# FFN up projection by one level of Strassen's algorithm, down projection accumulated over all of k in PSUM

## The chip, the cores and the metric

The kernel runs on one core of one Trainium2 chip. Its time is device microseconds of one execution. Three runs of the kernel before gave a median of 1679.16 us.

## The reference, cut to what matters

One decoder layer on 1024 tokens with a model width of 1024. A first part (modulated LayerNorm, gated linear attention and sliding-window attention side by side, output projection, LayerNorm) makes `x`. The change concerns what follows:

```python
h2 = layer_norm(x) * (1.0 + scale2) + shift2
u = h2 @ w_up[l]                                  # (1024, 1024) @ (1024, 5632)
up = jnp.pad(u, ((0, 0), (CONV_W - 1, 0), (0, 0)))
u = conv_b[l] + sum(conv_w[l, t] * up[:, t:t + S] for t in range(CONV_W))
u_gate, u_val = jnp.split(u, 2, axis=-1)          # 2816 each
f = jax.nn.gelu(u_gate, approximate=False) * u_val
x = layer_norm_affine(ALPHA * x + gate2 * (f @ w_down[l]), ln2_g[l], ln2_b[l])
```

## The kernel before, in words

**Precision.** Every large product is made of three matmuls: each operand is split into a high part `hi` (rounded to fp32r by a copy) and a low part `lo` (the difference), and hi·hi, hi·lo and lo·hi are accumulated. For weights, `Stream.emit_to` (L236) loads a 128x512 piece into `wst` (4 buffers), ScalarE writes `whi` (L250), VectorE writes `wlo` (L251); of each of these there are 8 buffers. For activations `to_half` does the same after a transpose (L392 to L401): ScalarE applies the modulation, VectorE copies hi, POOL subtracts lo.

**Order of TensorE.** It is written out by hand: `unit` (L329) issues the matmuls of one product, eight k tiles with three matmuls each, and after each k tile `run_due` issues what `at` has deferred until a running estimate of TensorE's time has passed. Within the other engines a scheduler orders instructions when the kernel is built, by their place in the program and by when their inputs should be ready.

**Before the FFN.** The last output projection (`o_unit` with 512 columns, 8 token tiles) is followed per token tile by `ln_a` (the first LayerNorm, into `x1[t]`) and `ln_b` (the normed copy `xn2[t]`). `h2_part` then makes `h2`, the transposed and split input, in two halves of 512 tokens. `ada_part(3, kt)` accumulates gate2 on VectorE (L603, L605: 16 pieces of 128x512), 2.5 us apart on the estimate.

**FFN.** The 2816 hidden units are 22 tiles of 128. `up_part(i, hf)` makes the gate and value products of tile i for one half of the tokens: two times 24 matmuls of 128x512, with the result in PSUM. `conv` reads PSUM: ScalarE takes the last tap and the bias (L1091), VectorE the other two (L1093, L1096); then Gelu (L1115), the product (L1118) and the split of f into `fh` (ScalarE, L1119) and `fl` (POOL, L1120). `down_piece` (L1130) multiplies f of one tile by its down weights for one token tile and one half of the columns: three matmuls into a PSUM bank, which VectorE adds to `x1` (L1145). The 16 pieces of tile v-2 are laid between the matmuls of `up_part(v)`. The down weights are multiplied by gate2 on POOL (L248) before they are split. The last three tiles (`N_LAST`) share one accumulation per piece and run at the end, each token tile followed by `finish` (L1147): the second LayerNorm on VectorE, its rstd on POOL (L369, L370), one scaling on ScalarE (L1158), one addition on POOL (L1159) and the store. SBUF keeps `x1` throughout, in the 8 buffers `y`.

```python
        for j in range(2):
            if tags is not None:
                us[i, j, hf] = ps1(tags)
            elif hf == 0:
                w2 = ps2()
                us[i, j, 0], us[i, j, 1] = w2[:, 0:512], w2[:, 512:1024]
            ch_unit(h2, hf, up_id[i], slice(128 * j, 128 * j + 128), us[i, j, hf], lambda: evac(j))
```

PSUM has 8 banks: two `pj`, two `m`, and two `w2` of two banks each.

Of the kernel before, what the change touches and what calls it, by code (L numbers as in the profile page):

```python
# [9 lines left out]
F32 = mybir.dt.float32  # L10
# [8 lines left out]
P = 128  # L19
S = 1024  # L20
# [12 lines left out]
N_LAST = 3  # L33
MOD_PE = 1
ADA3_D = 10.0
# [6 lines left out]
# ------------------------------------------------------------------ host layout  # L42
# [19 lines left out]
def _layout(a):  # L62
# [44 lines left out]
    return dict(x=a["x"][0], pos=pos, wlra=wlra, wbig=wbig, wdn=wdn, ada1=ada1, ada2=ada2, cst=cst, pv=pv, sm=sm,  # L107
# [3 lines left out]
_NAMES = ["x", "pos", "wlra", "wbig", "wdn", "ada1", "ada2", "cst", "pv", "sm", "lr", "rows"]  # L111


# ------------------------------------------------------------------ device program
@with_exitstack
def hybrid_layer_kernel(ctx: ExitStack, tc: tile.TileContext, x, pos, wlra, wbig, wdn, ada1, ada2, cst, pv, sm, lr,
# [9 lines left out]
    sq = ctx.enter_context(tc.tile_pool(name="sq", bufs=3))  # L126
    ps = ctx.enter_context(tc.tile_pool(name="ps", bufs=2, space=PSUM))
# [10 lines left out]
    sm_sb = cp.tile([P, 16 + 8 + 256], F32, name="sm_sb")  # L138
    pos_sb = cp.tile([P, NT], I32, name="pos_sb")
# [4 lines left out]
    ccum = cp.tile([P, 256], F32R, name="ccum")  # L144
# [12 lines left out]
    ring = cp.tile([P, P], F32, name="ring")  # L157
# [3 lines left out]
    diag = cp.tile([P, P], F32, name="diag")  # L161
# [14 lines left out]
    # ---------------- silu(c)  # L176
# [47 lines left out]
    # ---------------- weight stream  # L224
    class Stream:
# [988 lines left out]
```

## Time and profile before

| | us |
|---|---|
| three runs | 1677.97, 1679.16, 1681.36 |
| span of the profiled execution | 1677.0 |
| first matmul of the FFN | 916.7 |
| start of the last matmul | 1662.7 |

The profiled execution's own time is shown as its span, from its first to its last instruction; the median of the runs is 2.2 us above it. On the timelines a row gives start, duration, engine, line, operation, output and inputs, shape and count, and in brackets the idle time before it and what ended that. Neighbouring instructions of one engine overlap a little in these records, so the pitch from start to start is shorter than the duration.

### The profile page before, as it was taken

What the parts mean: (1) busy time and instruction counts of PE and PEld (TensorE: products, weight loads), DVE (VectorE), ACT (ScalarE), POOL (GpSimd) and SP (SyncE); (2) the same over time, 40 slices, a digit from 0 to 9 for tenths busy, and PEclk for the clock granted to TensorE, in tenths of its full rate; (3) what the DMA queues carried; (4) which work ended last, traced back from release to release, by engine and by line L of the source; (5) the groups of instructions that cost most, each with busy time, mean ns of one, the idle gap of its engine ahead of it and who ended that gap; (6) DMA issues with size and microseconds to landing.
All of it is one profiled execution on the core that took longest, in us unless ns stands there. A gap on an engine that the chain in (4) does not pass through costs nothing.

```text
span 1677.0 us, 28106 instructions
## 1 busy us (share of the span) xinstructions
PE 1619.8 (97%) x10777; PEld 1433.1 (85%) x10778; DVE 1079.8 (64%) x2278; ACT 658.6 (39%) x1590; POOL 504.0 (30%) x702
## 2 busy tenths in 40 slices
PE   5899999999999999999998899999999999999996
PEld 4899999998999989989996688888888888888885
DVE  7766666675645545536658876666666666666658
ACT  5565555554535544445313433222322222232222
POOL 5523222232623614415216521111111111111217
PEclk9999999999999999999999999999999999999998
DMA  7501000114123032111141422111211121112112
GB/s 245 163 24 36 27 27 27 33 46 121 57 61 116 27 101 89 52 51 33 51 131 39 139 68 65 44 39 46 62 44 38 51 63 39 38 50 64 38 38 101
DMA packets 58761, 108.28 MB, mean 65 GB/s; under 512 B 6641, under 2 KB 9201, under 8 KB 58626
## 3 DMA queue, kind: packets, MB, share of 16 engines
q1 hardware_dynamic: 58626, 106.49, 21.0%
q8 instruction: 84, 1.38, 0.3%
q14 instruction: 51, 0.42, 0.1%
HBM read 102.27 MB, written 4.19 MB: 63 GB/s over the span
## 4 chain that ended last, share of the span: by engine, by line
PE 86%; DVE 6%; POOL 4%; ACT 1%; issue 1%; DMA 1%; SPq 0%; DVEq 0%; POOLq 0%; ACTq 0%
PE pj L346 10%; PE pj L348 10%; PE pj L347 10%; PE w L361 9%; PE w L363 9%; PE w L362 9%; PE m L1139 6%; PE pj L1139 6%; DVE acc L530 2%; PE m L719 2%; PE pj L361 2%; PE pj L362 2%; PE pj L363 2%; PE m L758 2%; POOL y L1159 1%
## 5 line engine op out<-in xcount | busy, mean ns | idle before, releaser
L346 PE MATMUL pj<-whi,hh 128*128 128x256 f32 (+1 forms) x1296 | 373.2, 288 | 0.0
L348 PE MATMUL pj<-whi,hl 128*128 128x256 f32 (+1 forms) x1296 | 366.9, 283 | 0.0
L347 PE MATMUL pj<-wlo,hh 128*128 128x256 f32 (+1 forms) x1296 | 366.7, 283 | 0.0
L361 PE MATMUL w<-h2h,whi 128*128 128x512 f32 x672 | 266.7, 397 | 0.0
L362 PE MATMUL w<-h2l,whi 128*128 128x512 f32 x672 | 263.9, 393 | 1.0 <-POOL h2l L401 1.0
L363 PE MATMUL w<-h2h,wlo 128*128 128x512 f32 x672 | 264.4, 393 | 0.0
L346 PEld LDWEIGHTS pj<-whi,hh 128*128 128x128 f32 x1296 | 248.3, 192 | 0.6 <-issue 0.2
L347 PEld LDWEIGHTS pj<-wlo,hh 128*128 128x128 f32 x1296 | 246.5, 190 | 0.6 <-issue 0.2
L348 PEld LDWEIGHTS pj<-whi,hl 128*128 128x128 f32 x1296 | 246.1, 190 | 0.0
L251 DVE TENSOR_TENSOR wlo<-wst,whi 128x512 fp32r<-128x512 f32 (+1 forms) x200 | 145.2, 737 | 96.4 <-ACT whi L250 95.3
L1120 POOL TENSOR_TENSOR fl<-cv,fh 128x512 fp32r<-128x512 f32 x44 | 57.3, 1302 | 488.1 <-ACT fh L1119 473.3
L250 ACT CAST whi<-wst 128x512 fp32r<-128x512 f32 (+1 forms) x208 | 127.2, 620 | 152.9 <-DMA wst<-in_wbig 106.3
L362 PEld LDWEIGHTS w<-h2l,whi 128*128 128x128 f32 x672 | 126.7, 189 | 31.7 <-POOL h2l L401 1.8
L363 PEld LDWEIGHTS w<-h2h,wlo 128*128 128x128 f32 x672 | 126.4, 188 | 30.6
L361 PEld LDWEIGHTS w<-h2h,whi 128*128 128x128 f32 x672 | 126.4, 188 | 29.7 <-issue 0.2
L1145 DVE TENSOR_TENSOR y<-y,m 128x512 f32<-128x512 f32 x152 | 104.0, 684 | 71.7 <-PE m L1139 69.8
L1091 ACT ACTIVATE cv<-w,pv_sb 128x512 f32<-128x512 f32 x84 | 65.3, 777 | 214.6 <-PE w L363 214.2
L1093 DVE SCALAR_TENSOR_TENSOR cv<-w,pv_sb,cv 128x511 f32<-128x511 f32 (+1 forms) x168 | 125.2, 745 | 33.6 <-ACT cv L1091 32.3
L1145 DVE TENSOR_TENSOR y<-y,pj 128x512 f32<-128x512 f32 x152 | 104.2, 685 | 65.5 <-PE pj L1139 65.4
L248 POOL TENSOR_TENSOR wst<-wst,gate 128x512 f32<-128x512 f32 x44 | 58.7, 1338 | 79.6 <-DMA wst<-in_wdn 56.3
L698 POOL TENSOR_SCALAR_AFFINE_SELECT pch<-ph 128x512 f16<-128x512 f16 x32 | 20.5, 640 | 195.0 <-ACT ph L693 195.0
L675 ACT ACTIVATE ss<-ss,nm 128x128 f32<-128x128 f32 x128 | 49.9, 391 | 39.7 <-DVE nm L672 39.7
(402 smaller groups left out, 3526.2 us busy)
## 6 DMA issues: line engine op xcount, KB each, us to landing
wst<-in_wbig SPq DMA_DIRECT2D x200, 256.0 KB, 2.8
aw<-in_ada SPq DMA_DIRECT2D x96, 256.0 KB, 3.3
wst<-in_wdn SPq DMA_DIRECT2D x44, 256.0 KB, 2.6
y<-in_x SPq DMA_DIRECT2D x8, 512.0 KB, 9.0
out<-y SPq DMA_DIRECT2D x16, 256.0 KB, 2.0
xt<-in_x SPq DMA_DIRECT2D x8, 256.0 KB, 2.6
th<-in_x SPq DMA_DIRECT2D x13, 128.0 KB, 2.1
wst<-in_wlra SPq DMA_DIRECT2D x4, 272.0 KB, 2.7
```

Source lines behind the costliest of these rows:

```text
L250: act.copy(out=hi, in_=st)
L251: lo_eng.tensor_tensor(out=lo, in0=st, in1=hi.bitcast(F32), op=ALU.subtract)
L346: pe.matmul(acc, lhsT=lh, rhs=wh, start=kt == 0 if start is None else start, stop=False)
L347: pe.matmul(acc, lhsT=lh, rhs=wl, start=False, stop=False)
L348: pe.matmul(acc, lhsT=ll, rhs=wh, start=False, stop=kt == NK - 1 if stop is None else stop)
L361: pe.matmul(acc, lhsT=wh, rhs=ah[:, :, kt, :], start=(kt == 0), stop=False)
L362: pe.matmul(acc, lhsT=wh, rhs=al[:, :, kt, :], start=False, stop=False)
L363: pe.matmul(acc, lhsT=wl, rhs=ah[:, :, kt, :], start=False, stop=(kt == NK - 1))
L1091: act.activation(out=c_, in_=u, func=AF.Identity, scale=wv[:, 2:3], bias=bv)
L1093: dve.scalar_tensor_tensor(out=c_[:, lag:512], in0=u[:, 0:512 - lag], scalar=wv[:, 2 - lag:3 - lag], in1=c_[:, lag:512], op0=ALU.mult, op1 ...
L1139: pe.matmul(acc, lhsT=l_[:, ts_], rhs=r_[:, 0, :], start=(n == 0), stop=(n == 3 * len(blk) - 1))
L1145: dve.tensor_tensor(out=xs, in0=xs, in1=acc, op=ALU.add)
```

## The change

Twenty of the 22 gate/value tile pairs (all but the first two, `N_CLASSIC`) take Strassen's algorithm on 2x2 blocks: gate and value channels are the two column blocks, k tiles 0-3 and 4-7 the blocks of k, the two token halves the blocks of tokens. There are seven products (`product`, four k tiles with three matmuls each) per tile in place of eight such blocks. `combine` makes the sums of activation blocks (`tt_[2..4]`; a fourth is written over `h2`, `t1f`) once; `up_step` makes the sums of weight blocks per tile on POOL and splits seven weight operands; `tile_of` adds the products up, into `ug` and `uv` in SBUF. The convolution now works on 1024 tokens at a time and reads SBUF. f is written to HBM (`fd`), x1 too (`x1d`). A second stage then reads f and the down weights for each half `s` of the tokens and accumulates all 22 tiles in 8 PSUM banks, four token tiles by two column halves; `finish` multiplies by gate2. The modulation pieces `ada_part(3, kt)` start at 60 and come 6 us apart. Some constants get a pool of their own that is closed before the FFN; nothing else changes ahead of it.

```diff
-N_LAST = 3
+N_CLASSIC = 2
+B_FIRST = 3
-ADA3_D = 10.0
+ADA3_D = 60.0
+ADA3_P = 6.0
 ADA_D = 5.0
 LN_D = 5.0
 H2_D, H2_P = 12.0, 1.5
...
     wdn = a["w_down"][0].reshape(NFF, P, 2, 512).transpose(0, 2, 1, 3)
...
+    fd = tc.dram_tile([NFF, P, S], F32, name="fd")
     ps = ctx.enter_context(tc.tile_pool(name="ps", bufs=2, space=PSUM))
...
         for w_ in ids:
...
+        sp.dma_start(x1d[t], z)
...
+        keep = None
+        if hf == 1:
+            if kt % 2 == 0:
+                b1f.append(yp.tile([P, D], F32, name="b1f", tag="y"))
+            keep = b1f[kt // 2][:, 512 * (kt % 2):512 * (kt % 2) + 512].rearrange("p (a b) -> p a b", a=4)
+        to_half(h2, hf, kt, xn2[4 * hf:4 * hf + 4], mods[:, 3], mods[:, 2], s4, "xt", ps1("m"), True, 3, keep)
 
...
+    hqctx = ExitStack()
+    tt_ = {}
+    raws, wq, steps = {}, [], []
+
+    def conv(u, ch):
+
         wv = pv_sb[:, 40 + 3 * ch:43 + 3 * ch]
         bv = pv_sb[:, 40 + 6 * NFF + ch:41 + 6 * NFF + ch]
-        c_ = fa.tile([P, 512], F32, name="cv", bufs=4)
+        c_ = yp.tile([P, S], F32, name="cv", tag="y")
         act.activation(out=c_, in_=u, func=AF.Identity, scale=wv[:, 2:3], bias=bv)
         for lag in (1, 2):
-            dve.scalar_tensor_tensor(out=c_[:, lag:512], in0=u[:, 0:512 - lag], scalar=wv[:, 2 - lag:3 - lag],
-                                     in1=c_[:, lag:512], op0=ALU.mult, op1=ALU.add)
-            if hf == 1:
-                dve.scalar_tensor_tensor(out=c_[:, 0:lag], in0=prev[:, 512 - lag:512], scalar=wv[:, 2 - lag:3 - lag],
-                                         in1=c_[:, 0:lag], op0=ALU.mult, op1=ALU.add)
+            dve.scalar_tensor_tensor(out=c_[:, lag:S], in0=u[:, 0:S - lag], scalar=wv[:, 2 - lag:3 - lag],
+                                     in1=c_[:, lag:S], op0=ALU.mult, op1=ALU.add)
         return c_
...
+    def hidden(i, ug, uv):
+        cg = conv(ug, i)
+        act.activation(out=cg, in_=cg, func=AF.Gelu)
+        cv = conv(uv, i + NFF)
+        dve.tensor_tensor(out=cv, in0=cg, in1=cv, op=ALU.mult)
+        sp.dma_start(fd[i], cv)
...
+    def classic_part(i, hf):
+            us[i] = [yp.tile([P, S], F32, name="u", tag="y") for _ in range(2)]
+        for j in range(2):
+            ids = up_id[i][2 * j:2 * j + 2]
+            ws.get(ids[-1], 2)
+            acc = ps2()[:, 0:512] if j else ps1()
+            ch_unit(h2, hf, ids, slice(0, P), acc, lambda: act.copy(out=us[i][j][:, 512 * hf:512 * hf + 512], in_=acc))
+        if hf == 1:
+            hidden(i, *us.pop(i))
+
+    def pair(src):
+        hi, lo = (wp.tile([P, 4, P], F32R, name=n_, tag=n_) for n_ in ("whi", "wlo"))
+        act.copy(out=hi, in_=src)
+        dve.tensor_tensor(out=lo, in0=src, in1=hi.bitcast(F32), op=ALU.subtract)
+        wq.append((hi, lo))
+
+    def load(i):
+        r = raws[i] = []
+        for j in range(4):
+            t_ = (wp.tile([P, 4, P], F32, name="wst", tag="wst", bufs=4) if j < 2 else
+                  hq.tile([P, 4, P], F32, name="raw", tag="raw", bufs=5))
+            r.append(t_)
+        for j in (0, 2, 3, 1):
+            sp.dma_start(r[j], wup[i, j].rearrange("p (k c) -> p k c", k=4))
...
+    def up_step(i, n):
+
+        if n == 0 and i not in raws:
+            load(i)
+        if n == 2 and i + 1 < NFF:
+            load(i + 1)
+        r = raws[i]
+        a11, a12, a21, a22 = r[0:4]
+        if n == 0:
+            pair(a11)
+        elif n == 1:
+            s1 = hq.tile([P, 4, P], F32, name="raw", tag="raw", bufs=5)
+            r.append(s1)
+            pool.tensor_tensor(out=s1, in0=a21, in1=a22, op=ALU.add)
+            pool.tensor_tensor(out=a21, in0=a11, in1=a21, op=ALU.subtract)
+            pool.tensor_tensor(out=a11, in0=s1, in1=a11, op=ALU.subtract)
+            pair(a11)
+        elif n == 2:
+            pair(a12)
+            pool.tensor_tensor(out=a12, in0=a12, in1=a11, op=ALU.subtract)
+        elif n == 6:
+            pair(a12)
+            raws.pop(i)
+        else:
+            pair((a21, r[4], a22)[n - 3])
+
+    for i in range(N_CLASSIC, NFF):
+        steps.extend((i, n) for n in range(7))
+
+    def prep_to(n):
+        while len(wq) <= min(n, len(steps) - 1):
+            up_step(*steps[len(wq)])
+
+    def views(hl, kt):
...
+    def product(n, acc, b, start, evac):
+        prep_to(n + 7)
+        wh, wl = wq[n]
+        wq[n] = ()
+
+        def mm(kt):
+            bh, bl = b(kt)
+            go = dict(skip_group_check=not start)
+            pe.matmul(acc, lhsT=wh[:, kt, :], rhs=bh, start=start and kt == 0, stop=False, **go)
+            pe.matmul(acc, lhsT=wh[:, kt, :], rhs=bl, start=False, stop=False, **go)
+            pe.matmul(acc, lhsT=wl[:, kt, :], rhs=bh, start=False, stop=kt == 3, **go)
+
+        unit(mm, 0.69, evac, 4)
+
+    def tile_of(i):
+        n0 = 7 * (i - N_CLASSIC)
+        half = lambda hf, k0: lambda kt: (h2[hf][0][:, :, k0 + kt, :], h2[hf][1][:, :, k0 + kt, :])
+        comb = lambda m: lambda kt: (tt_[m][0][:, kt, :], tt_[m][1][:, kt, :])
+        ug, uv = (yp.tile([P, S], F32, name="u", tag="y") for _ in range(2))
+        g0, g1, v0, v1 = ug[:, 0:512], ug[:, 512:S], uv[:, 0:512], uv[:, 512:S]
+        a, c = ps1("pj"), ps1("m")
+        w2 = ps2()
+        b, d = w2[:, 0:512], w2[:, 512:1024]
+        p1 = hq.tile([P, 512], F32, name="p1", bufs=1)
+        add = lambda out_, x_, y_: dve.tensor_tensor(out=out_, in0=x_, in1=y_, op=ALU.add)
+        product(n0, a, half(0, 0), True, lambda: act.copy(out=p1, in_=a))
+        product(n0 + 1, b, comb(2), True, lambda: add(g1, b, p1))
+        product(n0 + 2, a, half(0, 4), False, lambda: act.copy(out=g0, in_=a))
+        product(n0 + 3, b, comb(3), False, lambda: add(v0, b, p1))
+        product(n0 + 4, c, half(1, 0), True, lambda: add(v1, c, v0))
+        product(n0 + 5, d, comb(4), True, lambda: add(v0, d, v0))
+        product(n0 + 6, c, half(1, 4), False, lambda: add(g1, c, g1))
+        hidden(i, ug, uv)
+
+    def split_to(hl, src):
+        act.copy(out=hl[0], in_=src)
+        dve.tensor_tensor(out=hl[1], in0=src, in1=hl[0].bitcast(F32), op=ALU.subtract)
+
+    t1f = []
+
+    def combine(kt):
+
+        sub = lambda e, out_, x_, y_: e.tensor_tensor(out=out_, in0=x_, in1=y_, op=ALU.subtract)
+        part = lambda hf, k_: [hl[:, :, k_, :] for hl in h2[hf]]
+        b12, b22 = (b1f[k_ // 2][:, 512 * (k_ % 2):512 * (k_ % 2) + 512].rearrange("p (a b) -> p a b", a=4)
+                    for k_ in (kt, kt + 4))
+        new = lambda: hq.tile([P, 4, P], F32, name="raw", tag="raw", bufs=5)
+        dst = lambda m: [hl[:, kt, :].rearrange("p (a b) -> p a b", a=4) for hl in tt_[m]]
+        t3, t4 = new(), new()
+        b11, b21 = part(0, kt), part(0, kt + 4)
+        sub(dve, t3, b22, b12)
+        split_to(dst(3), t3)
+        sub(dve, b12, b12, b11[0].bitcast(F32))
+        sub(dve, b12, b12, b11[1].bitcast(F32))
+        sub(dve, b22, b22, b12)
+        split_to(dst(2), b22)
+        sub(dve, t4, b21[0].bitcast(F32), b22)
+        dve.tensor_tensor(out=t4, in0=t4, in1=b21[1].bitcast(F32), op=ALU.add)
+        split_to(dst(4), t4)
+        t1f.append((b12, part(1, kt)))
+
...
+    for kt in range(NK):
+        at(ADA3_D + ADA3_P * kt, 0.0, lambda kt=kt: ada_part(3, kt))
+    at(ADA3_D + ADA3_P * 8, 1.7, lambda: ada_end(3))
+    for hf in range(2):
+        for i in range(N_CLASSIC):
+            classic_part(i, hf)
+            if (hf, i) == (0, N_CLASSIC - 1):
+                s4ctx.close()
+                factx.close()
+                hq = hqctx.enter_context(tc.tile_pool(name="hq", bufs=1, side="right", reuse_waits="tile"))
+                for m in (2, 3, 4):
+                    tt_[m] = [hq.tile([P, 4, 512], F32R, name=f"t{m}{hl}") for hl in "hl"]
+                for kt in range(4):
+                    combine(kt)
+                prep_to(5)
+    for src, hl in t1f:
+        split_to(hl, src)
+    for i in range(N_CLASSIC, NFF):
+        tile_of(i)
+    hqctx.close()
+
+
+    fq = ctx.enter_context(tc.tile_pool(name="fq", bufs=2, side="right", reuse_waits="tile"))
+    g2b, b2b = (fq.tile([P, D], F32, name=n_, bufs=1) for n_ in ("g2b", "b2b"))
...
+    def down_prep(s, i):
+        st = fq.tile([P, 512], F32, name="fst")
+        sp.dma_start(st, fd[i][:, 512 * s:512 * s + 512])
+        slot = f_slot(s, i)
+        split_to(slot, st)
+        w = []
+        for hf in range(2):
+            st = wp.tile([P, 512], F32, name="wst", tag="wst", bufs=4)
+            sp.dma_start(st, wdn[i, hf])
+            src = wp if (2 * len(dq) + hf) % 12 < 8 else fq
+            hl = [src.tile([P, 512], F32R, name=n_, tag=n_, bufs=8 if src is wp else 4) for n_ in ("whi", "wlo")]
+            split_to(hl, st)
+            w.append(hl)
+        dq.append((slot, w))
+
+    def down_to(n):
+        while len(dq) <= min(n, 2 * NFF - 1):
+            down_prep(len(dq) // NFF, len(dq) % NFF)
+
...
+    def finish(s, tl):
+        t = 4 * s + tl
+        z = xts.pop(t)
+        st = sq.tile([P, 2, 6], F32, name="bst")
+        for hf in range(2):
+            cs = slice(512 * hf, 512 * hf + 512)
+            tmp = fq.tile([P, 512], F32, name="fst")
+            dve.tensor_tensor(out=tmp, in0=banks[s, tl][hf], in1=gate[:, cs], op=ALU.mult)
+            dve.scalar_tensor_tensor(out=z[:, cs], in0=z[:, cs], scalar=ALPHA, in1=tmp, op0=ALU.mult, op1=ALU.add)
+            dve.bn_stats(out=st[:, hf], in_=z[:, cs])
+        mv = sq.tile([P, 2], F32, name="mv")
+        dve.bn_aggr(out=mv, in_=st.rearrange("p a b -> p (a b)"))
+        rs = rstd(mv, LN_EPS)
+        for hf in range(2):
+            cs = slice(512 * hf, 512 * hf + 512)
+            zs = z[:, cs]
+            dve.scalar_tensor_tensor(out=zs, in0=zs, scalar=mv[:, 0:1], in1=g2b[:, cs], op0=ALU.subtract, op1=ALU.mult)
+            if t == NT - 1:
+                dve.scalar_tensor_tensor(out=zs, in0=zs, scalar=rs, in1=b2b[:, cs], op0=ALU.mult, op1=ALU.add)
+            else:
+                act.activation(out=zs, in_=zs, func=AF.Identity, scale=rs)
+                pool.tensor_tensor(out=zs, in0=zs, in1=b2b[:, cs], op=ALU.add)
+            sp.dma_start(out[t * P:(t + 1) * P, cs], zs)
+
+    order = (0, 2, 3, 1)
+    for s in range(2):
+        n_last = B_LAST[s]
+        down_to(s * NFF + B_FIRST - 1)
+        for tl in order:
+            if tl in (0, 1):
+                banks[s, tl] = [ps1("m" if tl else "pj") for _ in range(2)]
+            else:
                 w2 = ps2()
-                us[i, j, 0], us[i, j, 1] = w2[:, 0:512], w2[:, 512:1024]
-            ch_unit(h2, hf, up_id[i], slice(128 * j, 128 * j + 128), us[i, j, hf], lambda: evac(j))
-
-    def down_piece(blk, t, hf):
-        ts_ = slice(t * P, (t + 1) * P)
-        cs = slice(512 * hf, 512 * hf + 512)
-        acc = ps1("m" if hf else "pj")
-        n = 0
-        for i in blk:
-            fh, fl = fts[i]
-            wh, wl = ws.tiles[dn_id[i][hf]]
-            for l_, r_ in ((fh, wh), (fh, wl), (fl, wh)):
-                pe.matmul(acc, lhsT=l_[:, ts_], rhs=r_[:, 0, :], start=(n == 0), stop=(n == 3 * len(blk) - 1))
-                n += 1
-        xs = x1[t][:, cs]
-        if blk[0] == 0:
-            dve.scalar_tensor_tensor(out=xs, in0=xs, scalar=ALPHA, in1=acc, op0=ALU.mult, op1=ALU.add)
-        else:
-            dve.tensor_tensor(out=xs, in0=xs, in1=acc, op=ALU.add)
```

## Rows read from the trace of the kernel before

**Rows 1.** Busy time of each engine, from the page

```profile
PE 1619.8 (97%) x10777; PEld 1433.1 (85%) x10778; DVE 1079.8 (64%) x2278; ACT 658.6 (39%) x1590; POOL 504.0 (30%) x702
```

**Rows 2.** Chain that ended last, by engine, from the page

```profile
PE 86%; DVE 6%; POOL 4%; ACT 1%; issue 1%; DMA 1%; SPq 0%; DVEq 0%; POOLq 0%; ACTq 0%
```

**Rows 3.** Stretches: from:to, length, busy us (instructions), clock, DMA share, GB/s

```profile
900.00:960.00 60.00, 51.62 (x231) 40.50 (x229) 50.95 (x74) 27.56 (x37) 37.98 (x33) 0.93 0.38 110
...
936.00:940.00 4.00, 4.00 (x17) 3.21 (x16) 2.55 (x4) 1.16 (x2) 3.17 (x3) 0.61 0.54 177
...
1100.00:1300.00 200.00, 200.00 (x865) 162.13 (x864) 130.29 (x216) 53.62 (x84) 31.41 (x24) 1.00 0.17 48
...
1664.00:1677.00 13.00, 0.00 (x0) 0.00 (x0) 9.19 (x12) 1.39 (x3) 7.68 (x8) 0.58 0.32 122
```

**Rows 4.** Waits of TensorE from 900 us on: total, times, longest

```profile
PE m L392 <- ACT xt L395: 4.1, 1, 4.1
PE m L392 <- ACT fh L1065: 3.3, 1, 3.3
PE w L362 <- POOL h2l L401: 1.0, 2, 0.7
```

**Rows 5.** Timeline of VectorE in the steady stage

```profile
1102.24 0.68 DVE L1145 TENSOR_TENSOR y<-y,m 128x512 f32<-128x512 f32 x1
1102.84 0.68 DVE L1145 TENSOR_TENSOR y<-y,pj 128x512 f32<-128x512 f32 x1
```

**Rows 6.** VectorE by line and form: busy us, mean ns, idle before

```profile
L251 DVE TENSOR_TENSOR wlo<-wst,whi 128x512 fp32r<-128x512 f32 x196 | 142.4, 737 | 96.1 <-ACT whi L250 95.1 <-POOL hl L401 0.2
...
L1058 DVE SCALAR_TENSOR_TENSOR y<-y,mv,g1b 128x1024 f32<-128x1024 f32 x8 | 10.3, 1287 | 0.0
```

**Rows 7.** ScalarE by line and form

```profile
L250 ACT CAST whi<-wst 128x512 fp32r<-128x512 f32 x204 | 124.7, 619 | 152.1 <-DMA wst<-in_wbig 106.3 <-PE pj L348 26.7 <-PE pj L362 10.4
...
L1065 ACT ACTIVATE fl<-y,nb,rs 128x1024 f32<-128x1024 f32 x4 | 5.0, 1245 | 26.2 <-POOL nb L386 26.2
```

**Rows 8.** Costliest groups, from the page: POOL

```profile
L248 POOL TENSOR_TENSOR wst<-wst,gate 128x512 f32<-128x512 f32 x44 | 58.7, 1338 | 79.6 <-DMA wst<-in_wdn 56.3
```

**Rows 9.** Timeline of VectorE beside POOL

```profile
932.57 2.07 DVE L605 SCALAR_TENSOR_TENSOR gate<-aw,csil,gate 128x512 f32<-128x512 f32 x3
...
941.04 2.44 DVE L605 SCALAR_TENSOR_TENSOR gate<-aw,csil,gate 128x512 f32<-128x512 f32 x2
...
944.39 0.73 DVE L1093 SCALAR_TENSOR_TENSOR cv<-pj,pv_sb,cv 128x510 f32<-128x510 f32 x1
```

**Rows 10.** Timeline of POOL in the same stretch

```profile
941.20 1.73 POOL L401 TENSOR_TENSOR h2l<-xt,h2h 128x512 fp32r<-128x512 f32 x1 [0.37 <-DVE h2h L398]
944.55 1.30 POOL L401 TENSOR_TENSOR h2l<-xt,h2h 128x512 fp32r<-128x512 f32 x1 [1.62 <-DVE h2h L398]
```

**Rows 11.** Timeline of TensorE: start, length, form, idle before it

```profile
915.86 0.63 PE L347 MATMUL pj<-wlo,yTh 128*128 128x512 f32 x1
916.29 0.63 PE L348 MATMUL pj<-whi,yTl 128*128 128x512 f32 x1
...
934.70 0.33 PE L392 MATMUL m<-ident,fh 128*128 128x128 f32 x1 [3.35 <-ACT fh L1065]
```

**Rows 12.** Transfers: form, count, size, us to landing

```profile
wst<-in_wbig SPq DMA_DIRECT2D x200, 256.0 KB, 2.8
...
out<-y SPq DMA_DIRECT2D x16, 256.0 KB, 2.0
```

**Rows 13.** Timeline of the end, all engines

```profile
1662.72 0.40 PE L1139 MATMUL m<-whi,fl 128*128 128x512 f32 x1
...
1668.47 2.93 POOL L1159 TENSOR_TENSOR y<-y,wst 128x512 f32<-128x512 f32 x2 [0.83 <-ACT y L1158]
...
1672.72 1.42 DVE L1156 SCALAR_TENSOR_TENSOR y<-y,rs,wst 128x512 f32<-128x512 f32 x2 [0.77 <-POOL rs L370]
```

More of the change, by code (lines that the diff above doesn't have):

```diff
@@ L327, in run_due, with unit @@
             fn()
-    def unit(mm, cost, evac):
-        for kt in range(NK):
+    def unit(mm, cost, evac, n=NK):
+        for kt in range(n):
             mm(kt)
             now[0] += cost
-            if kt < NK - 1:
+            if kt < n - 1:
                 run_due()
@@ L419, in hybrid_layer_kernel @@
     y = [None] * NT
[L420 removed]
+    lrT = gp.tile([17, S], F32, name="lrT")
     pool.memset(lrT, 1.0)
@@ L1180, in hybrid_layer_kernel @@
-    at(0.0, 0.0, lambda: None)
-    now[0] += 100.0
-    run_due()
-    last = [i for i in range(NFF) if i not in dn_early]
-    for i in last:
-        ws.get(dn_id[i][-1], 0)
-    g2b = [wp.tile([P, 512], F32, name="wst", tag="wst", bufs=4) for _ in range(2)]
-    b2b = [wp.tile([P, 512], F32, name="wst", tag="wst", bufs=4) for _ in range(2)]
-    for hf in range(2):
-        sp.dma_start(g2b[hf], rows[4][:, 512 * hf:512 * hf + 512])
-        sp.dma_start(b2b[hf], rows[5][:, 512 * hf:512 * hf + 512])
@@ new lines, in hybrid_layer_kernel, with f_slot @@
+    for src, hl in t1f:
[5 more added lines that the diff above has]
+    g2b, b2b = (fq.tile([P, D], F32, name=n_, bufs=1) for n_ in ("g2b", "b2b"))
+    dq, fs, banks, xts = [], {}, {}, {}
+    def f_slot(s, i):
+        if s == 0 and i < B_FIRST:
+            e_ = yp.tile([P, 2, 512], F32R, name="fe", tag="y")
+            return e_[:, 0, :], e_[:, 1, :]
+        n = i - (0 if s else B_FIRST)
+        if n % 8 == 0:
+            if n == 0:
+                fs[s] = [[fq.tile([P, 8, 512], F32R, name="f" + hl, tag="f") for hl in "hl"]]
+            else:
+                fs[s].append([hp.tile([P, 8, 512], F32R, name="f" + hl, tag="h") for hl in "hl"])
+        return [hl[:, n % 8, :] for hl in fs[s][n // 8]]
@@ new lines, in down_to, with down_mm @@
+    def down_to(n):
+        while len(dq) <= min(n, 2 * NFF - 1):
+            down_prep(len(dq) // NFF, len(dq) % NFF)
+    def down_mm(s, i, tl, hf):
+        (fh, fl), w = dq[s * NFF + i]
+        wh, wl = w[hf]
+        ts_ = slice(tl * P, (tl + 1) * P)
+        acc = banks[s, tl][hf]
+        for n, (l_, r_) in enumerate(((fh, wh), (fh, wl), (fl, wh))):
+            pe.matmul(acc, lhsT=l_[:, ts_], rhs=r_, start=i == 0 and n == 0, stop=i == NFF - 1 and n == 2)
+    def finish(s, tl):
[21 more added lines that the diff above has]
+            sp.dma_start(out[t * P:(t + 1) * P, cs], zs)
@@ new lines, in hybrid_layer_kernel @@
+    order = (0, 2, 3, 1)
[6 more added lines that the diff above has]
+            else:
+                w2 = ps2()
+                banks[s, tl] = [w2[:, 0:512], w2[:, 512:1024]]
+            for hf in range(2):
+                for i in range(B_FIRST):
+                    down_mm(s, i, tl, hf)
+            down_to(s * NFF + B_FIRST + 1)
+        for i in range(B_FIRST, NFF - n_last):
+            down_to(s * NFF + i + 3)
+            for tl in order:
+                for hf in range(2):
+                    down_mm(s, i, tl, hf)
+        if s == 0:
+            sp.dma_start(g2b, rows[4])
+            sp.dma_start(b2b, rows[5])
+        for tl in range(4):
+            t = 4 * s + tl
+            xts[t] = yp.tile([P, D], F32, name="xr", tag="y")
+            sp.dma_start(xts[t], x1d[t])
+        for tl in order:
+            down_to(s * NFF + NFF + B_FIRST - 1)
+            for hf in range(2):
+                for i in range(NFF - n_last, NFF):
+                    down_mm(s, i, tl, hf)
+            finish(s, tl)
```

125 lines of the change are left out of this document (30 added, 95 removed).

## The prediction

> **What bounds the kernel now.** I read the busy times first: TensorE works 97% of the span, VectorE 64% [rows 1]. The chain that ended last agrees: 86% of it is TensorE [rows 2]. As a share can hide stages, I then cut the FFN into stretches. From 1100 to 1300 TensorE is busy for 200.00 of 200 us at a granted clock of 1.00, with 865 matmuls, all of 128x512: one per 0.2312 us, the unit of the whole sum. VectorE works 130 us of these 200, ScalarE 54, POOL 31. TensorE stands still only at the edges: 8.4 us in 900 to 960 and the end from 1664 on [rows 3]. Its waits there are two for the normed tiles and their transposes, 4.1 and 3.3 us, and 1.0 us for POOL [rows 4]. So a matmul less in the FFN is 0.2312 us less, as long as the other engines keep up.
>
> **Matmuls removed.** Before, a tile pair takes 2 (gate, value) x 2 (halves) x 8 x 3 = 96 matmuls in the up projection. A Strassen tile takes 7 x 4 x 3 = 84. Twenty tiles save 240, all on the path: -55.5 us. The down projection keeps its 22 x 16 x 3 = 1056. The additions to `x1` and the POOL multiplications by gate2 vanish too, and are worth nothing: TensorE waits for neither.
>
> **VectorE in a Strassen tile.** TensorE needs 84 x 0.2312 = 19.4 us. VectorE subtracts seven lows and adds five times from PSUM, 128x512 each at a pitch of 0.60 [rows 5]: 7.2 us. It makes four taps and one product, 1024 wide, at about 1.2 (1.287 with the overlap, [rows 6]): 6.0. Together 13.2, or 68%. ScalarE has seven casts at 0.62, two copies, two taps and a Gelu at up to 1.24 [rows 7]: 9.3 us. POOL has four additions, at 1.34 by the nearest row [rows 8]: 5.4 us. No engine is over its time, but POOL and VectorE disturb each other. Three modulation updates, which read two tiles in SBUF, take 2.07 us alone; two take 2.44 beside one POOL subtraction, 1.06 more than 2 x 0.69 [rows 9, 10]. The tap that reads PSUM stays at 0.73 while POOL starts beside it [rows 9, 10]. After the change the taps read `ug` and `uv` in SBUF, the disturbed form; four POOL operations may thus cost up to 4.2 us per tile: 17.4 of 19.4, still covered.
> The Trainium skill, "GPSIMD Engine Reference", section "Specifications", says that POOL shares its SBUF interfaces with VectorE and contends with instructions that have two SBUF inputs. The trace agrees, with the 2.44 us above. By that rule the new taps lose time where the row of the present tap shows none; with the present row the wait of the next paragraph would be 0.
>
> **The wait at each tile's turn.** The second and the fourth product share a bank, so the first addition must be through 3 x 2.77 = 8.3 us after the tile starts. Ahead of it on VectorE stands `hidden` of the tile before: last addition 0.7, ScalarE's tap 1.24, two taps 2.4, Gelu 1.2, product 1.2, then the addition 0.6: 7.3 us, if the value half, complete one product earlier, is convolved by then. That leaves 1.0 us. Two POOL operations in it, 2 x 1.06, make it 1.1 us late. I take 0.5 us, the middle, for 20 tiles: +10 us. Ends: 0, and +40 for 2 us per tile.
>
> **The start.** `combine` is 36 VectorE operations (nine for each of four k tiles): 21.6 us. Its inputs come with the second half of h2, from about 945 us on (POOL subtracts the lows of the third and fourth of its eight k tiles at 941.20 and 944.55 [rows 10]). The two classic tiles have their 192 x 0.2312 = 44.4 us and the transposes from 916.7 on, so TensorE wants the first Strassen product at about 966. VectorE has 22 us until then and must also do the last casts (2.8), meet POOL four times (4.2) and make the first low (0.6): 29 us, 7 late. The fourth sum's splits and both classic tiles' taps, some 14 us, then press on the first tile: 2 more. After the wait of 3.35 us at 934.7 the granted clock was 0.61 over 4 us [rows 3, 11]: 1 more. Together +10. Ends: 0, if the scheduler spreads it, and +25, about all of `combine` uncovered. Against this, the taps of the first half (L1093, L1118) no longer stand between the last LayerNorm's steps, and the 3.3 us wait [rows 4] shrinks: -2.5, between 0 and -3.3.
>
> **The modulation pieces.** 16 updates at 0.69 = 11 us move into the first two and a half Strassen tiles: 4.4 per tile on 13.2. With all POOL contention that is 21.8 against 19.4, 6 us late in all; without any, 0. I take +3.
>
> **The down stage and its turns.** A step is 24 matmuls, 5.55 us. VectorE and ScalarE split three pieces: 1.8 and 1.9 us. Three loads of 256 KB are 142 GB/s; 177 were moved at a DMA share of 0.54 [rows 3], and a load lands in 2.8 us [rows 12], so the four `wst` buffers cover it. On SP the writes of f wait for `hidden`, with the next weight loads behind them; these are needed seven products (19 us) later. At the turn to the second half, four `finish` (5.3 us of VectorE each) and nine splits (5.4) are 27 us within eight groups of 18 matmuls, 33 us. If this cover fails, TensorE waits for a bank. I take +2 for both turns, ends 0 and +8.
>
> **The end.** Now the last matmul starts at 1662.7, and 14 us follow, since POOL needs 4.98 us per token tile (its two additions 2.5, the rstd and waits) against 4.16 of matmuls and falls behind [rows 13]. After the change a token tile has 30 matmuls, 6.9 us. Then the tail is one chain: 0.6 + 0.7 + 0.6 + 0.2 on VectorE, 1.6 rstd, 0.7 scaling, 2.5 POOL, 2.0 store [rows 12], with waits about 10. So -4, between 0 and -5.
>
> **Sum.** -55.5 + 10 + 10 - 2.5 + 3 + 2 - 4 = -37.0. Against the span of 1677.0 that is 1640.0, and the 2.2 us between span and median make it **1642.2 us**. About 0.2%, 3.4 us, can be told from no change.
>
> **Rivals.**
> - Nothing waits: start, turns of tiles and modulation cost 0. For it: all engines are under their time. Against: the start lacks 7 us by its rows. Then -55.5 - 2.5 + 2 - 4 = -60: 1619. Chance 0.17.
> - The tile's turn costs 1.5 us instead of 0.5, with a third POOL operation in it: +20, 1662. Chance 0.15. At 2.35 us per tile the 37 us are used up ((37 + 10) / 20); close to that point, no change, 0.03.
> - Slower: VectorE does all of `hidden`, the value taps included, ahead of the bank's addition. 0.6 + 0.6 + 2.4 + 2.4 + 1.2, all four POOL operations (4.2), one low and the addition (1.2) are 12.6 us against 8.3: 4.3 per tile, 3.8 over my 0.5, +76: 1718. For it: program order ranks `hidden` first. Against: `uv` is complete a product earlier. It decides from 2.35 us per tile on. Chance 0.08.
> - Slower: TensorE's clock swings in the down stage, where every three matmuls go to another of eight banks. At half clock the pitch is 0.43 [rows 11]; half of 1056 matmuls would cost 528 x 0.20 = +105: 1747. Against: in 1100 to 1300 each three matmuls of a down piece also change bank, and the clock is 1.00 [rows 3]. Chance 0.02.
> The Trainium skill, "TensorE: Matmul & The Clock Gate", section "A second HAM failure mode: psum-queue depth-cycling", describes such swings, with TensorE idling briefly between groups; no row here shows one.
>
> **How the numbers follow.** The forecast has 0.55. Faster: 0.55 + 0.17 + 0.15 = 0.87; same 0.03; slower 0.10. The low end, 1618, takes in the first rival; the high end, 1672, takes the second with another 10 us for the start's bound. That holds about 8 in 10.
>
> **What would show it.** Right: 2928 FFN matmuls at a pitch of 0.231; a wait of 5 to 10 us ahead of the first Strassen product, ended by a VectorE low or sum; waits below 1 us at the fourth product of a tile, ended by an addition from PSUM; a clock of 1.00 in the down stage. Wrong: VectorE over 95% busy in the Strassen stage, waits of over 2 us in every tile, or loads that TensorE waits for in the down stage.

## The result, and the profile after

The changed kernel takes 1705.1 us (1703.6 to 1706.5) against 1679.8 us: a ratio of 1.0151 [1.0137, 1.0166], 25 us slower. The profiled execution has a span of 1702.6 us. Busy times of the engines and the chain that ended last, from the page of after:

```profile
PE 1585.9 (93%) x10537; PEld 1399.3 (82%) x10538; DVE 1070.3 (63%) x2080; ACT 736.6 (43%) x1692; POOL 500.7 (29%) x694
...
PE 27%; DVE 8%; issue 4%; ACT 2%; DMA 1%; POOL 0%; POOLq 0%; ACTq 0%; DVEq 0%
```

The shares of the chain add up to 42% only, so nothing below rests on it. Against [rows 1] TensorE has 240 matmuls less, and is busy for 93% of the span instead of 97%. No other engine is near its limit over the whole span, so the time lies in waits of TensorE and in what follows them. The listed waits from 890 us on, after (total us, times, longest), against [rows 4]:

```profile
PE w L1179 <- DVE u L1195: 34.8, 18, 4.7
PE m L613 <- DVE gate L596: 12.4, 2, 11.1
PE w L1179 <- ACT whi L1122: 9.4, 1, 9.4
PE m L382 <- ACT xt L386: 4.4, 2, 4.2
PE pj L1296 <- ACT fe L1206: 4.4, 2, 3.8
PE pj L1296 <- DVE fe L1207: 3.1, 1, 3.1
PE m L382 <- ACT fh L1059: 3.1, 1, 3.1
PE w L1181 <- DVE wlo L1123: 2.4, 1, 2.4
```

L1179 and L1181 are the matmuls of a Strassen product, L613 the last step of gate2, L1296 the down products, L382 the transposes ahead of the FFN. [rows 4] begins at 900: the 3.1 us for `fh` here lie at 899 and stand before the change as well, at 898. The stretches of after, with the columns of [rows 3]:

```profile
960.00:980.00 20.00, 10.58 (x47) 8.41 (x45) 19.96 (x23) 13.80 (x21) 5.95 (x3) 0.87 0.16 50
980.00:1000.00 20.00, 12.96 (x37) 9.55 (x38) 17.46 (x20) 6.33 (x12) 9.45 (x5) 0.71 0.33 108
1060.00:1083.00 23.00, 10.63 (x30) 6.38 (x29) 13.74 (x16) 5.04 (x6) 2.95 (x2) 0.65 0.29 94
1100.00:1200.00 100.00, 92.47 (x395) 73.61 (x394) 71.94 (x82) 39.67 (x57) 25.38 (x19) 1.00 0.24 76
1500.00:1600.00 100.00, 100.00 (x434) 81.22 (x433) 54.97 (x81) 32.35 (x53) 19.11 (x16) 1.00 0.40 132
```

From 1100 to 1200, the steady Strassen stage, TensorE starts 395 matmuls where [rows 3] has 865 in 200: a tile takes 21.2 us, not 19.4. The down stage (1500 to 1600) is full, at a clock of 1.00. After the long waits the clock is low for a while: 0.71 and 0.65. That shows in the work, too: TensorE is busy 34 us less than before, while 240 matmuls at 0.230 us are 55. Matmuls that took longer make up the other 21 us; from 980 to 1000, for one, 37 of them take 12.96 us, where 37 x 0.230 is 8.5.

One steady tile, on VectorE and ScalarE (two timelines of after; the seventh product ends, and the next tile's first addition is L1195 at 1148.01):

```profile
1138.95 0.69 DVE L1195 TENSOR_TENSOR u<-m,u 128x512 f32<-128x512 f32 x1 [1.50 <-PE m L1181]
...
1141.02 5.33 DVE L1096 SCALAR_TENSOR_TENSOR cv<-u,pv_sb,cv 128x1023 f32<-128x1023 f32 x4 [0.78 <-ACT cv L1094]
1146.28 0.68 DVE L1123 TENSOR_TENSOR wlo<-wst,whi 128x512 fp32r<-128x512 f32 x1
1146.88 1.21 DVE L1104 TENSOR_TENSOR cv<-cv 128x1024 f32<-128x1024 f32 x1
1148.01 0.68 DVE L1195 TENSOR_TENSOR u<-w,p 128x512 f32<-128x512 f32 x1
```

```profile
1139.74 2.38 ACT L1094 ACTIVATE cv<-u,pv_sb 128x1024 f32<-128x1024 f32 x2 [0.40 <-DVE u L1195]
```

ScalarE takes both last taps back to back, only after the seventh product's addition; VectorE then does all four of its taps in one run, and the addition comes 9.06 us after the one before. TensorE meets it at the fourth product (timeline of TensorE, after):

```profile
1148.75 0.50 PE L1179 MATMUL w<-t3h,whi 128*128 128x512 f32 x1 [1.51 <-DVE u L1195]
```

### The profile page after: what moved, and what is told of

The parts are those of the page before. It is cut to its first block, busy times and chain, and to the rows that moved or that the text cites. A ratio compares the mean times of both kernels' runs of the same rounds, so it can differ in the third digit from the quotient of the medians.

```text
span 1702.6 us, 28004 instructions
## 1 busy us (share of the span) xinstructions
PE 1585.9 (93%) x10537; PEld 1399.3 (82%) x10538; DVE 1070.3 (63%) x2080; ACT 736.6 (43%) x1692; POOL 500.7 (29%) x694
## 5 line engine op out<-in xcount | busy, mean ns | idle before, releaser
L1096 DVE SCALAR_TENSOR_TENSOR cv<-u,pv_sb,cv 128x1023 f32<-128x1023 f32 (+1 forms) x88 | 119.3, 1409 | 13.4 <-ACT cv L1094 13.2
L253 DVE TENSOR_TENSOR wlo<-wst,whi 128x512 fp32r<-128x512 f32 (+1 forms) x116 | 84.8, 748 | 43.3 <-ACT whi L252 43.0
L1207 DVE TENSOR_TENSOR wlo<-wst,whi 128x512 fp32r<-128x512 f32 x88 | 60.0, 699 | 59.6 <-ACT whi L1206 59.2
L1122 ACT CAST whi<-raw 128x512 fp32r<-128x512 f32 x60 | 37.0, 619 | 137.8 <-PE w L1180 69.1
L1122 ACT CAST whi<-wst 128x512 fp32r<-128x512 f32 x80 | 49.2, 620 | 106.7 <-PE w L1180 60.1
L252 ACT CAST whi<-wst 128x512 fp32r<-128x512 f32 (+1 forms) x124 | 75.2, 619 | 43.9 <-PE pj L338 27.9
L1206 ACT CAST whi<-wst 128x512 fp32r<-128x512 f32 x88 | 53.2, 619 | 75.2 <-PE m L1296 55.9
L1179 PE MATMUL w<-t3h,whi 128*128 128x512 f32 x80 | 35.8, 447 | 34.8 <-DVE u L1195 34.8
L1179 PE MATMUL pj<-h2h,whi 128*128 128x512 f32 x160 | 64.5, 403 | 0.0
L1296 PE MATMUL w<-whi,fl 128*128 128x512 f32 x164 | 64.5, 393 | 0.0
L1296 PE MATMUL w<-whi,fh 128*128 128x512 f32 x164 | 64.4, 393 | 0.0
```

The lines of the kernel that those rows point to most:

```text
L252: act.copy(out=hi, in_=st)
L253: lo_eng.tensor_tensor(out=lo, in0=st, in1=hi.bitcast(F32), op=ALU.subtract)
L1096: dve.scalar_tensor_tensor(out=c_[:, lag:S], in0=u[:, 0:S - lag], scalar=wv[:, 2 - lag:3 - lag], in1=c_[:, lag:S], op0=ALU.mult, op1=ALU.add)
L1122: act.copy(out=hi, in_=src)
L1179: pe.matmul(acc, lhsT=wh[:, kt, :], rhs=bh, start=start and kt == 0, stop=False, **go)
L1207: dve.tensor_tensor(out=hl[1], in0=src, in1=hl[0].bitcast(F32), op=ALU.subtract)
```

## The experiments: the turn of each tile

**Another bank for the fourth product.** `b` and `d` are the two banks of one `w2` tile. The fourth product goes to `d`, which nothing uses at that time, the sixth to `b`. This leaves the second product out of the value half.

```diff
-        product(n0 + 3, b, comb(3), False, lambda: add(v0, b, p1))
+        product(n0 + 3, d, comb(3), True, lambda: add(v0, d, p1))
...
-        product(n0 + 5, d, comb(4), True, lambda: add(v0, d, v0))
+        product(n0 + 5, b, comb(4), True, lambda: add(v0, b, v0))
```

> The changed kernel, with the fourth and the sixth product of a tile exchanging their banks, so that the fourth writes a bank that was read long before. Theory (the fourth product waits for one addition, which stands on VectorE behind the whole hidden-unit work of the tile before): the 15 waits of 1.5 us and their restarts of 0.3 go, and most of the three longer ones of 3.4 to 4.7 us near the start with the half clock after them, 27 to 38 us in all: 1667 to 1678 us. Rival (VectorE has too much work per tile, whatever the order): the wait turns up at another product and under 10 us are won: 1695 or more.

Measured: 1705.4 us, 1.0147 [1.0130, 1.0163], no gain. The waits of this run stay at the fourth product, though the bank it writes isn't the one that is read:

```profile
PE w L1179 <- DVE u L1195: 34.9, 18, 4.6
```

**The addition ahead of `hidden`.** `hidden(i)` is issued behind the next tile's first addition.

```diff
         product(n0 + 1, b, comb(2), True, lambda: add(g1, b, p1))
+        if held:
+            hidden(*held.pop())
...
-        hidden(i, ug, uv)
+        held.append((i, ug, uv))
```

> The changed kernel with its banks as they are, but the convolution, Gelu and product of a tile are placed in the program behind the first addition of the next tile. Theory (it is the order on VectorE): the same 27 to 38 us as with the banks exchanged, 1667 to 1678 us, and the addition runs directly after its product. Rival (the work of VectorE that is pushed back now delays later additions or the weights): 1690 or more, with waits at the sixth or seventh product or at the weights.

Measured: 1698.1 us, 1.0109 [1.0093, 1.0125]. The first addition is now prompt, and the wait stands at the sixth product (into `d`) instead, until 0.73 us after the fourth product's addition, which reads `b`, has started. TensorE and VectorE of this run:

```profile
1147.04 0.50 PE L1179 MATMUL w<-t4h,whi 128*128 128x512 f32 x1 [1.60 <-DVE u L1197]
```

```profile
1138.76 5.88 DVE L1096 SCALAR_TENSOR_TENSOR cv<-u,pv_sb,cv 128x1023 f32<-128x1023 f32 x4 [0.20 <-ACT cv L1094]
...
1146.31 0.68 DVE L1197 TENSOR_TENSOR u<-w,p 128x512 f32<-128x512 f32 x1
```

In both runs a product into one bank waits for the read of the other. The wait goes by the whole two-bank PSUM tile. Whether the chip asks for this, or only the waits that are written into the program when it is built, no run shows.

**A PSUM tile of its own.** The fourth product gets a second `w2` tile and is added to `g1`, which already holds the first two, so the same products are summed.

```diff
-        w2 = ps2()
-        b, d = w2[:, 0:512], w2[:, 512:1024]
+        w2, w3 = ps2(), ps2()
+        b, d, e = w2[:, 0:512], w2[:, 512:1024], w3[:, 0:512]
...
-        product(n0 + 3, b, comb(3), False, lambda: add(v0, b, p1))
+        product(n0 + 3, e, comb(3), True, lambda: add(v0, e, g1))
```

> The changed kernel, but the fourth product of a tile opens a bank of a second PSUM tile (two of the double-bank tiles per Strassen tile) and is added to the upper gate half in place of being accumulated on the second product; the operations keep their number and sizes. Theory (a matmul waits for the readers of its whole PSUM tile, both banks of it, so the exchange of banks inside one tile changed nothing and the late order only moved the wait to the sixth product): no wait of 1.5 us is left at the fourth or sixth product, 27 us less from the steady tiles and up to 10 more near the start: 1668 to 1679 us. Rival (VectorE does not keep up with a tile in 19.4 us): a wait of over 1 us per tile at another product: 1690 or more.

Measured: 1667.6 us, 0.9928 [0.9910, 0.9946], 37.5 us below the changed kernel. The steady stage is full, with VectorE at 76%:

```profile
1100.00:1200.00 100.00, 100.00 (x435) 81.27 (x434) 76.17 (x88) 43.84 (x61) 31.98 (x22) 1.00 0.25 83
```

**No Strassen.** All 22 tiles plain, with the round trip of f through HBM and the new down stage kept (240 matmuls more).

```diff
-    for i in range(N_CLASSIC, NFF):
-        tile_of(i)
+    for i in range(N_CLASSIC, NFF):
+        for hf in range(2):
+            classic_part(i, hf)
```

> All 22 tiles by the plain product with their result through HBM, then the second stage as in the changed kernel: the change without Strassen, with 240 matmuls more. Theory (the second stage itself costs the wait at its start, 7.6 us, and about 2 us at half clock, and nothing else; the wait for the last normed tile, 3.4 us, is gone): 1680 to 1690 us against 1679 before. Rival (the round trip through HBM and the loading of the down weights twice cost more): over 1695 us, with waits for loads inside the second stage.

Measured: 1676.9 us, 0.9982 [0.9973, 0.9991]. The rest of the change is worth 3 us; what makes it slow comes in with the Strassen tiles, whose 55.5 us of saved matmuls are given back and 28 us more.

## The experiments: the modulation pieces

**Later and further apart.** `ADA3_D` 60 to 110, `ADA3_P` 6 to 12.

> The changed kernel with the modulation pieces of gate2 starting at 110 in place of 60 on the estimate and coming 12 us apart in place of 6. Theory (their loads share the wst buffers with the raw weights of two tiles, so the loads come late, TensorE waits 12.4 us for gate2 and loses about 2 us at half clock, and the turns of two tiles take 2 us longer each and lose the clock): 16 to 22 us less, 1683 to 1689 us. Rival (the loads come late at any pace, because the SP queue waits for a buffer each time): a wait of 5 us or more for gate2 stays, only later: 1697 or more.

Measured: 1702.9 us, 1.0138 [1.0121, 1.0155]; the wait for the gate is 9.4 us, only at another time. The changed kernel's timelines show the chain (POOL, SP, VectorE, TensorE): a load of gate2's weights takes a `wst` buffer that the Strassen weights also use, and it comes free only with the last of a tile's sums on POOL. The update of gate2 on VectorE waits for that load, and TensorE for the update.

```profile
1071.28 1.26 POOL L1154 TENSOR_TENSOR wst<-wst 128x512 f32<-128x512 f32 x1 [7.82 <-DVE wlo L1123]
```

```profile
1072.56 3.62 SPq L586 DMA_DIRECT2D aw<-in_ada  x2
```

```profile
1075.08 0.75 DVE L596 SCALAR_TENSOR_TENSOR gate<-aw,csil,gate 128x512 f32<-128x512 f32 x1 [4.02 <-DMA aw<-in_ada]
```

```profile
1075.88 2.08 PE L613 MATMUL m<-gate,ones 128*128 128x512 f32 x2 [11.07 <-DVE gate L596]
```

Of the waits of the SP queue between 900 and 1100 (total us, times, longest), these are the ones of gate2's loads for that sum on POOL:

```profile
SPq L586 <- POOL wst L1154: 13.3, 4, 5.3
```

**Buffers of their own.** The pieces of gate2 are loaded as 512 KB into `y` buffers, one load in place of two.

```diff
+        if v == 3:
...
+            aw = yp.tile([P, D], F32, name="aw", tag="y")
+            sp.dma_start(aw, ada2[v * NK + kt])
+            for hf in range(2):
+                cs = slice(512 * hf, 512 * hf + 512)
+                ada_acc(aw[:, cs], cs, kt)
+            return
```

> The changed kernel with the modulation pieces of gate2 and their bias row loaded into the larger buffers that hold gate, value and hidden units, not into the wst buffers that the raw weights of two tiles hold. Theory (the wait for gate2 and the longer turns of the tiles before come from the four wst buffers): the 12.4 us wait for gate2 and its 2 us of half clock go, and 3 to 8 us around it: 1683 to 1691 us. Rival (VectorE or SP is late there for another reason, or the larger buffers are as scarce): over 1698 us.

Measured: 1685.6 us, 1.0030 [1.0017, 1.0044], 19.5 us below the changed kernel: more than the 12.4 us of the wait, around which the clock was 0.65 (1060 to 1083). No wait for the gate is left. The buffers and the number of loads changed together; that it is the buffers rests on the waits of the SP queue above.

**Both edits together.**

> Fourth product in a bank of its own and gate2's pieces loaded into buffers of their own, together. Theory (the tile's turn and the modulation's loads are two separate losses): 1705.1 - 37.5 - 19.5 = 1648 us, no wait of TensorE between 1020 and 1390 us over 1 us, and the waits left are those at the first Strassen tile (about 12 us) and at the first down products (7.5 us). Rival (the modulation's wait hid other work of the first tiles, which is late next): the gate's wait is replaced by waits for VectorE in the tiles before 1100 us, and the time stays over 1655.

Measured: 1650.0 us, 0.9822 [0.9808, 0.9835]: 55.1 us of the 57.0 that the two gave alone. Waits of 9.4 us (`whi`), 5.0 and 2.4 us in the first Strassen tiles, and 7.5 us at the first down products, stay.

## The experiments: the start, the down turn and the end

**The weights' first splits ahead of the sums.** `prep_to(1)` ahead of the four `combine(kt)`, in the changed kernel.

> The changed kernel with the first two weight operands of the first Strassen tile prepared ahead of the sums of activations in the program. Theory (the 9.4 us wait at the second product comes from its weight sum, which waits for a buffer that the activation sums hold and then for ScalarE's queue): 5 to 11 us less, 1694 to 1700 us. Rival (VectorE's backlog at the start only moves): the waits at the second and fourth product of the first tile add up to 14 us or more as now: under 3 us won.

Measured: 1704.5 us, 1.0143 [1.0126, 1.0160]. The wait for `whi` is gone, and its successors stand in its place:

```profile
PE w L1179 <- ACT t2h L1206: 8.4, 1, 8.4
...
PE w L1180 <- DVE t2l L1207: 1.5, 1, 1.5
```

**The classic tiles' `hidden` behind the first Strassen tile's additions** (on the kernel with both edits).

> As the kernel with both edits, but the convolution, Gelu and product of the two classic tiles (about 12 us of VectorE) stand behind the additions of the first Strassen tile. Theory (the wait ahead of the first Strassen tile is VectorE's and ScalarE's backlog, in which these stand ahead of the weights' first splits): the waits of 9.4 us for whi and 2.4 us for wlo fall below 3 us together, and the time is 8 to 12 us below that of the kernel with both edits. Rival (the backlog is the sums of activation blocks themselves, in whatever order): the waits move to the products with t2, t3 and t4 and the time stays within 3 us.

Measured: 1647.5 us, 0.9808 [0.9795, 0.9822], 2.4 us below it. The same again: 5.6 us for `whi` stay, and 6.5 us come up at the second tile.

```profile
PE w L1191 <- DVE u L1207: 6.5, 1, 6.5
PE w L1191 <- ACT whi L1134: 5.6, 1, 5.6
```

**The last tile's `hidden` behind the preparation of the first three down tiles** (in the changed kernel).

> The changed kernel with the convolution, Gelu and product of the last tile placed behind the preparation of the first three tiles of the down stage. Theory (ScalarE's and VectorE's splits of f stand behind the last tile's hidden units): the waits of 7.6 us at the start of the down stage fall below 3, and half clock of 2 us goes: 1696 to 1700 us. Rival (the loads of f are late, whatever the order): 5 us or more of waits stay: 1702 or more.

Measured: 1702.1 us, 1.0133 [1.0115, 1.0150]. The first two down tiles no longer wait for their casts (0.99 and 0.26 us), but the third waits 4.5 us: `fst` has two buffers, so its load is issued only when VectorE's subtraction has read one (1437.09), and the cast waits for it until 1442.17.

**The same with a third load buffer** (on the kernel with both edits).

```diff
-        st = fq.tile([P, 512], F32, name="fst")
+        st = yp.tile([P, D], F32, name="fst2", tag="y")[:, 0:512] if s == 0 and i == 2 else fq.tile([P, 512], F32, name="fst")
```

> As the kernel with both edits, but the convolution, Gelu and product of the last tile stand behind the preparation of the first three down tiles, and the third f piece is loaded into a buffer of its own. Theory (the first down products wait because their casts queue behind the last tile's taps, and, in the run that moved only these, because the third load had no buffer): no wait of over 1.3 us at the first down products, and 6 to 8 us below the kernel with both edits. Rival (the loads themselves come too late, since they are issued only when the last tile's stage is closed): waits of 3 us or more stay, ended by the fe casts whose loads have just landed.

Measured: 1644.7 us, 0.9789 [0.9775, 0.9804]: 5.3 us below that kernel; waits of 3.0 and 0.6 us are left of 7.5.

**All edits so far.**

> All edits together. Theory (start, turn, modulation and down turn are separate terms): the gains of the two kernels add up, 1648 - 10 - 7 = 1631 us, with at most 10 us of TensorE's waits left from 960 us on. Rival (one of the start's waits only moves): 1638 to 1643.

Measured: 1642.0 us, 0.9774 [0.9761, 0.9788], with 20 us of waits from 960 us on: the rival's figure, as the start's waits only move.

**Three plain tiles** (on the one with the down turn mended), the third behind `combine`. The preparation of the first weights, `prep_to(5)`, moves behind the first half of that tile.

```diff
-N_CLASSIC = 2
+N_CLASSIC = 3
...
+    classic_part(N_CLASSIC - 1, 0)
+    prep_to(5)
+    classic_part(N_CLASSIC - 1, 1)
```

> As the kernel with the down turn mended (1644.7), but three plain tiles instead of two, the third of them behind the sums of activation blocks: 12 matmuls more (+2.8 us), 22 us more cover. Theory (the cover was too short for VectorE's sums as a whole): the waits of 9.4, 2.4 and 4.9 us around the first Strassen tile and its matmuls at half clock (some 3 us) go, and the time falls by 12 to 17 us, to 1628 to 1633. Rival (the chain of loads, POOL's sums, casts and subtractions of the first weights sets it, and moves with the first Strassen tile): a wait of 6 us or more stays ahead of that tile, and the time is 1642 to 1648.

Measured: 1634.4 us, 0.9738 [0.9725, 0.9751]: 10.4 us less in spite of 2.8 us more matmuls. No wait is left ahead of the first Strassen tile's second product, as the theory said, but the gain falls short of its 12 to 17 us. All of TensorE's waits between 960 and 1060 us in this run:

```profile
PE pj L1190 <- ACT p L1209: 5.6, 1, 5.6
PE m L1190 <- DVE u L1208: 1.2, 1, 1.2
```

The 5.6 us are the copy of the first product, which ScalarE takes up behind a plain tile's Gelu, which itself waits 5.3 us for VectorE's taps: the rest of the same backlog.

**The shortened last steps in the last token tile.** The order of the token tiles is 0, 2, 3, 1; the changed kernel does scaling and addition in one VectorE operation for number 3, the third of the last four.

```diff
-            if t == NT - 1:
+            if s == 1 and tl == order[-1]:
```

> As the kernel with three plain tiles, but the last scaling and addition are one VectorE operation in the token tile that is really the last one, instead of in the third of the last four. Theory (the end was missed because this step stands in the wrong token tile, where it delays the last one): the time from the start of the last matmul to the end falls from about 13.6 to 10 us, and the whole by 3 to 4 us. Rival (the store and the statistics set the end): less than 1 us.

Measured: 1632.8 us, 0.9724 [0.9711, 0.9737], the lowest median of all. It is 1.6 us below the kernel with three plain tiles, but single runs of the two overlap (1631.0 to 1633.5 and 1632.6 to 1638.5). From the start of the last matmul to the end it is 11.4 us (1617.97 to 1629.4) against 13.5 (1617.27 to 1630.8): 2.1 us, between theory and rival. In the changed kernel VectorE starts that operation (L1316) just when the last products are ready, and comes to them (L1305) only at 1691.66:

```profile
1689.04 0.40 PE L1296 MATMUL m<-whi,fl 128*128 128x512 f32 x1
```

```profile
1689.73 1.41 DVE L1316 SCALAR_TENSOR_TENSOR xr<-xr,rs,b2b 128x512 f32<-128x512 f32 x2
1691.06 0.68 DVE L1307 BATCH_NORM_STATS2 bst<-xr 128x6 f32<-128x512 f32 x1
1691.66 0.67 DVE L1305 TENSOR_TENSOR fst<-m,gate 128x512 f32<-128x512 f32 x1
...
1694.07 1.41 DVE L1314 SCALAR_TENSOR_TENSOR xr<-xr,mv,g2b 128x512 f32<-128x512 f32 x2
```

## Why the prediction was wrong

It said 1642.2 us and faster, with a chance of 0.10 for slower; it was 1705.1 and slower. By its own steps:

- **Matmuls removed: right.** 240 matmuls are gone. 435 in 100 us where nothing waits is 0.230 us each, and 240 of them are 55.2 us, against the 55.5 forecast.
- **Engine loads in a Strassen tile: right.** Without the wait VectorE is busy 76% of the tile's 19.4 us: 14.8 us, between the 13.2 and 17.4 of the prediction.
- **The turn of each tile: +10 forecast, 37.5 measured.** This is the step that decided. It let the value half be "convolved by then", as it is complete one product earlier. It isn't: on ScalarE the value half's tap stands behind the gate half's, as `hidden` has them, and that one waits for the seventh product. So all four VectorE taps fall between the two additions, 9.06 us apart. This is the mechanism of the slower rival (chance 0.08) at a lower price, 1.8 us per tile instead of 4.3, mostly because one POOL operation fell into the stretch, not four. On top came the first tiles with up to 4.7 us. The second rival had the price (1.5 us) but took it for the only loss.
- **POOL beside VectorE.** The four taps took 4.87 us at 1435.78 with no POOL operation beside them, and 5.33 us at 1141.02, where 0.67 us of a POOL subtraction (1140.39 to 1141.69) fall within them: 0.46 us. In the run with the addition ahead of `hidden` almost a whole subtraction (1138.69, 1.29 us) falls within them (1138.76), and they took 5.88 us: 1.01 us more, close to the 1.06 us of [rows 9, 10]. So the price held, and the number of operations in the turn was lower. By the Trainium skill ("GPSIMD Engine Reference", section "Specifications") the two contend for SBUF where VectorE has two SBUF inputs; the trace agrees, with these 0.46 and 1.01 us. It is a small part of the turn.
- **The modulation pieces: +3 forecast, 19.5 measured.** The step counted VectorE's updates and no buffer. The pieces' loads share the four `wst` buffers with `load(i)`, and there a weight block stays until POOL has made the tile's last sum from it. That lifetime is in the diff (`a11` lies in `wst` and is read by the sum of step 2); the step on loads in the down stage counted these four buffers, this one didn't.
- **The start: +10 forecast, about 20 measured** (13.2 us recovered by a third plain tile: the gain of 10.4 and its 2.8; 6.8 us of waits left). The mechanism was right, a VectorE that is behind (from 960 to 980 it is busy for 19.96 of 20 us); but the 14 us of taps and sums that press on the first tile were counted at 2 us. Two edits that changed only their order moved the wait.
- **The wait at the last LayerNorm: -2.5 forecast.** The 3.35 us wait at 934.7 [rows 11] is gone, as was said.
- **The turn to the down stage: +2 forecast, about 9 by the waits and the run that removed 5.3.** The cover was there for the steady stage and for the turn between halves (no wait after 1445 us); the first three f pieces, at a time when VectorE and ScalarE do the last tile's `hidden`, were not looked at, nor the two buffers of their loads.
- **The end: -4 forecast, -0.7 measured** (13.6 us from the last matmul's start, 14.3 before). The steps of the last token tile were the ones listed, and took about 10 us by the forecast. Two terms were short. VectorE was taken to be free when the last products are ready; it still works on the token tile before and comes to them 2.2 us later (1689.04 + 0.40, against 1691.66). And the last store was put at 2.0 us, while 3.4 us pass from POOL's last addition (1699.2) to the end. Moving the shortened steps to the last token tile took 2.1 us off this stretch.
- **The clock rival: rightly low.** Every three matmuls go to another bank in the down stage at a granted clock of 1.00 (1500 to 1600). The swings of the Trainium skill's "TensorE: Matmul & The Clock Gate", section "A second HAM failure mode: psum-queue depth-cycling", are not seen here; there was no idling between groups (TensorE busy for 100.00 of 100 us).

With the measured terms, taken from different kernels, the sum is -55.5 + 37.5 + 20 - 3.3 + 19.5 + 9 - 0.7 = +26.5, against 25.3 measured. The kernel with edits against the turn, the modulation's loads, the order at the start and the down turn takes 1642.0 us. That this is the forecast's figure is luck: quite other terms are in it, and it confirms nothing of the forecast's steps. Not tried: the value half's taps first in `hidden`, which would test the order within the turn alone; that the value half's taps come late because of ScalarE's order is read from the trace.

## What to carry to other kernels

A wait that comes once per tile is worth its price times all tiles, so write down the queue of each engine in program order between the two events, not what could be ready by then; an operation that is ready stands behind one that isn't. For every operation that is moved, list whose buffers it takes and who frees them, loads included: two of the four large losses were buffers (the two-bank PSUM tile at the turn, `wst` for gate2's loads), not engine time alone. A slack worked out in a steady stage says nothing of its first and last tile: there the neighbouring stage's backlog runs beside it.

## What was not expected of the hardware and the program

A product into one bank of a two-bank PSUM tile waits for the reads of the other bank: 34.9 us in all with `d` in the place of `b`, none in the steady stage with a tile of its own. And with two such tiles per Strassen tile, which leaves no second set for the next one, TensorE was still busy for 100.00 of 100 us: the separate tile was worth more than the double buffer.
